# Groups of seven products in the first gate and up block of FFN 2 and in the embedding's first pair of blocks, and six tiles for the heads' squares

## The chip, the cores and the metric

The kernel runs on one core of one Trainium2 chip. The metric is the device time of one execution in microseconds (us); lower is better. Before the change three runs took 1833.35, 1833.89 and 1834.02 us.

The core's engines work beside one another: TensorE (PE in the profile; its weight loads are PEld), VectorE (DVE), ScalarE (ACT), GpSimd (POOL) and SyncE (SP). SP issues most DMA transfers; POOL issues a few, among them the accumulating ones, which add into what they write. The on-chip memory is SBUF; TensorE writes its sums to PSUM.

## The reference, cut to what matters

One layer of a streaming encoder: 256 tokens, width 2048, everything in float32.

```python
x = x + 0.5 * swiglu(rms_norm(x, ffn1_norm), ffn1_w_gate, ffn1_w_up, ffn1_w_down)
h = rms_norm(x, mix_norm); proj = h @ w_in            # u | q | k | v
y_ssm = s5_mixer(u, ...)                              # with a gated linear unit at its end
y_sb = stick_breaking_attention(rms_norm(q), rms_norm(k), v)
x = x + concatenate([rms_norm(y_ssm), rms_norm(y_sb)]) @ w_out
x = x + 0.5 * swiglu(rms_norm(x, ffn2_norm), ffn2_w_gate, ffn2_w_up, ffn2_w_down)
gate = sigmoid(rms_norm(x, ple_norm) @ w_ple_gate)    # the embedding: 2048 x 2048
x = x + rms_norm((p @ w_ple_proj) * gate, ple_post_norm)
```

with `swiglu(h, g, u, d) = (silu(h @ g) * (h @ u)) @ d` and an inner width of 5632.

## The kernel before, in words

**Products in three passes.** Each float32 operand is split into a high part (rounded, by a cast on ACT, line 181) and a low part (what is left, a subtraction on DVE, line 184). A product is the sum of high x high, low x high and high x low: three matmuls where one would do in a lower precision. Weights come as quarters: four rows of 128 inputs by 512 columns, 1 MB in one `raw` tile. There are five such tiles; two of them hold `x` from time to time, and during the embedding all the time. A quarter is split in two halves of 128x1024 elements, into tiles `whi` and `wlo` (four of each; while a pool for sums is open, three more, `shi` and `slo`).

**Blocks.** The 256 tokens are two tiles of 128 rows. A block is 512 columns of output for all tokens, its inner dimension taken a quarter at a time: 2048 inputs are quarters 0 to 3. `gemm_half` (line 315) issues 12 matmuls of 128x128 by 128x512 for one half. `gemm_block` does one block; `gemm_pair` does two blocks with quarters 0 and 1 of the first, 0 and 1 of the second, then quarter 2 of each, then quarter 3 of each.

**Groups of seven products.** The class `Seven` (line 463) handles two blocks together, gate and up for instance. For one quarter, activations and weights make two 2x2 matrices of blocks, and the products of the two matrices are formed in Winograd's way, from seven products and some additions, not eight. The seven are numbered 1 to 7, and are issued in the order 1, 5, 6, 4, 2, 3, 7. `chunk` (line 504) loads both weight quarters, forms three sums of weights on DVE (`add`, line 501), a fourth by an accumulating DMA from SBUF to SBUF on POOL's queue (line 525, for product 7), and splits the seven weight operands. The sums of activations, called forms, are made once per quarter by `whole_rows` (line 443) and `sum_forms` (line 458). `column` does ordinary quarters for one of the two blocks into the same PSUM banks. The banks 1, 2, 4 and 5 are `acc` tiles of 512 columns (four exist); 6 and 7 share one `aux` tile of 1024 columns, 3 and 8 the other (two exist). A group thus uses all of PSUM, and afterwards `opened` and `gated` combine its banks by additions on DVE and a copy on ACT; a last addition takes in banks 3 and 8 (line 622).

In FFN 2's gate and up products, blocks 1 to 10 each use two groups (quarters 0 and 1) and ordinary columns for quarters 2 and 3. Block 0 uses `gemm_pair` and no group; after its gate half, the forms of quarters 0 and 1 are made for the later blocks. The embedding's gate blocks 0 and 1 use `gemm_pair`, and ACT applies the sigmoid right from PSUM (`gate_block`).

**Around these places.** `Normed` holds the normalised, transposed input: a block of `x` is turned on DVE (line 216), sent through SBUF by 16 small DMAs on SP's queue (line 229), and split with the gain (lines 191 and 193). The row scale from the mean of squares comes later, at the evacuation. In the mixer, the heads' outputs and the gated unit's outputs are squared and summed by `add_square`: ACT squares into a tile `sqp` (two exist), POOL adds it to a total (line 1331). Of the totals `rms` makes a row scale (a sum by TensorE, small DVE operations, a square root on ACT), with which line 1464 evacuates the output projection's blocks.

**What sets the order.** The program is written with work put off by so many steps (`put_off`, `step`), and a planner then orders each engine's instructions by the program's order and by when it reckons that their inputs and tiles are there. Instructions wrapped in `pin` keep the program's order. At run time each queue is served in the planned order.

Of the kernel before, what the change touches and what calls it, by code (L numbers as in the profile page):

```python
# [33 lines left out]
def layer_kernel(ctx: ExitStack, tc: tile.TileContext, a: dict, shapes: dict, out: bass.AP):  # L34
# [32 lines left out]
    def get(pool, tag, width=1024, bufs=1):  # L67
        return pool.tile([P, width], F32, tag=tag, name=uid(tag), bufs=bufs)
# [486 lines left out]
    def ffn(i, xn, nxt, bg=None):  # L555
# [23 lines left out]
        for f in range(NF):  # L579
            if prep and f == early:  # L580
# [3 lines left out]
                sevens = pools.enter_context(sums_phase(f"sums{i}"))  # L584
                hp = pools.enter_context(phase(f"h{i}b"))
                sums = [sum_forms(sevens, whole_rows(sevens, xn(kb)), "h") for kb in range(2)]
            if sevens and f:
                sg, hh = com("sg"), com("h")
                gate_cols, up_cols = ([u[:, t * NB : (t + 1) * NB] for t in range(TT)] for u in (sg, hh))

                def opened(s, g=gate_cols, u=up_cols):
                    nc.scalar.copy(g[0], s.bank(1))
                    nc.vector.tensor_tensor(out=u[0], in0=s.bank(6), in1=g[0], op=ALU.add)
                    nc.vector.tensor_tensor(out=u[1], in0=s.bank(7), in1=u[0], op=ALU.add)

                def gated(s, g=gate_cols, u=up_cols, hh=hh):
                    for z, (ps, other) in enumerate(((s.bank(2), g[0]), (s.bank(4), u[1]))):
                        nc.vector.tensor_tensor(out=g[z], in0=ps, in1=other, op=ALU.add)
                        nc.scalar.activation(g[z], g[z], AF.Silu, scale=xn.rs(z))
                    v = hh.rearrange("p (t n) -> p t n", t=TT)  # L600
                    nc.vector.tensor_tensor(
                        out=v, in0=s.bank(5).unsqueeze(1).to_broadcast([P, TT, NB]), in1=v, op=ALU.subtract
                    )

                s = Seven(xn, lambda kb: sums[kb], ((wg, f * NB), (wu, f * NB)), sevens)
                two = f != early
                if f == early:
# [12 lines left out]
                put_off(0, gated, s)  # L620
                s.column(1, (2, 3) if two and f != early else (1, 2, 3), True)
                nc.vector.tensor_tensor(out=hh, in0=s.banks[3.8], in1=hh, op=ALU.add)
# [12 lines left out]
            if f == 0 and bg:  # L635
                warm_up(10)
                first = first_quarters(wg, xn)
            if f == 0 and not bg:
                both = gemm_pair(xn, ((wg, 0), (wu, 0)), KD)
                pg = next(both)  # L640
                sums = [sum_forms(sevens, whole_rows(sevens, xn(kb))) for kb in range(2)]
            else:
                pg = gemm_block(xn, wg, f * NB, KD, first)
            sg = com("sg")
            if f == 0 and bg:
# [6 lines left out]
            pu = gemm_block(xn, wu, f * NB, KD) if f or bg else next(both)  # L652
            if prep and f == 0:
                start(prep)
            hh = com("h")
# [669 lines left out]
    def add_square(pool, total, src, first):  # L1325
        if first:
            nc.scalar.activation(total, src, AF.Square)
        else:
            sq = get(pool, "sqp", T, 2)
            nc.scalar.activation(sq, src, AF.Square)  # L1330
            nc.gpsimd.tensor_tensor(out=total, in0=total, in1=sq, op=ALU.add)

# [180 lines left out]
            ple(n, t, gate, ps[t])  # L1513

    wg = a["w_ple_gate"][0]
    g0, g1 = (gate_block(ps) for ps in gemm_pair(npl, ((wg, 0), (wg, NB)), KD))
    proj_block(0, g0)
    proj_block(1, g1)
    proj_block(2, gate_block(gemm_block(npl, wg, 2 * NB, KD)))
    n = ND - 1  # L1520
    gate = com("h")
    gates = gemm_resident(npl, a["w_ple_gate"][0], n * NB, KD, fin, KD - 8)
    projs = gemm_resident(lambda k: pT, a["w_ple_proj"][0], n * NB, PD // P, fin, PD // P, 2)

    def add(t, n_, r):
        x, g = xt[t][n_], es[n_][:, t * NB : (t + 1) * NB]
# [54 lines left out]
    diag = fin.tile([P, P], F32, name="diag")  # L1581
# [96 lines left out]
```

## Time and profile before

| | |
|---|---|
| three runs | 1833.35, 1833.89, 1834.02 us (median 1833.89) |
| the profiled execution's own time | 1833.81 us |
| its span, from first to last instruction | 1831.7 us |
| TensorE busy | 1820.2 us, 8972 matmuls |
| VectorE busy | 1506.1 us |
| ScalarE busy | 1047.8 us |
| GpSimd busy | 95.7 us |
| granted TensorE clock | 0.999 |

The profile is of one execution. Times in its rows are microseconds from the span's start. A row of the timeline has the start, the duration, engine, line of the kernel, operation, output <- inputs, shape and count; in brackets stands how long the engine was idle before it, and what ended that wait. A matmul's duration includes its way through the array, so that neighbours overlap: their cost is the distance from start to start. Rows by stretch give the stretch, its length, and the busy time of each engine with its instructions, then the granted clock, the share of DMA busy and GB/s.

### The profile page before, as it was taken

The numbers are of one execution on the slowest core, as the hardware profiler recorded it, in microseconds if no ns is written. First come the engines' busy times: TensorE is split into PE (matmuls) and PEld (weight loads), VectorE is DVE, ScalarE is ACT, GpSimd is POOL, SyncE is SP. The second block draws the span as 40 slices with busy tenths as digits, with TensorE's granted clock in tenths as the row PEclk, the third lists the DMA queues.
The fourth block names the chain that finished last, engine by engine and source line by source line (L and its number), as shares of the span: only waits on it lengthen the run. The fifth ranks groups of instructions, "written<-read, shape, count | busy, mean of one in ns | idle before, by whom it ended". The sixth has DMA issues, their size and how long they took to land.

```text
span 1831.7 us, 24182 instructions
## 1 busy us (share of the span) xinstructions
PE 1820.2 (99%) x8972; PEld 1507.0 (82%) x8972; DVE 1506.1 (82%) x1771; ACT 1047.8 (57%) x1221; POOL 95.7 (5%) x145
## 2 busy tenths in 40 slices
PE   9999999999999999999999999999999999999998
PEld 7888888788888888888898888888888888888887
DVE  8967664999999996687566789999999999999565
ACT  7444443655566665365695566555565556666564
POOL 0011000000100000010021000000000010000000
PEclk9999999999999999999999999999999999999999
DMA  9889868677967676675636787887877787767563
GB/s 331 285 271 289 253 209 252 207 236 227 281 215 247 207 238 216 191 265 170 209 132 215 227 300 213 258 253 248 244 221 239 240 267 235 235 205 248 176 214 127
DMA packets 237639, 425.79 MB, mean 232 GB/s; under 512 B 27376, under 2 KB 51312, under 8 KB 237232
## 3 DMA queue, kind: packets, MB, share of 16 engines
q1 hardware_dynamic: 227824, 392.81, 64.6%
q0 software_dynamic: 8976, 30.02, 7.5%
q8 instruction: 70, 1.15, 0.2%
q10 hardware_dynamic: 720, 1.41, 0.2%
q14 instruction: 49, 0.40, 0.1%
HBM read 373.46 MB, written 11.93 MB: 210 GB/s over the span
## 4 chain that ended last, share of the span: by engine, by line
PE 91%; DVE 5%; DMA 2%; issue 1%; ACT 1%; SPq 0%; DVEq 0%; ACTq 0%
PE acc L322 18%; PE acc L327 18%; PE acc L323 18%; PE aux L323 6%; PE aux L322 6%; PE aux L327 6%; PE acc L497 3%; PE acc L494 3%; PE acc L495 3%; PE aux L497 2%; PE aux L494 2%; PE aux L495 2%; DVE wlo L184 1%; DVE slo L184 1%; DMA raw<-in_ffn_w_down 1%
## 5 line engine op out<-in xcount | busy, mean ns | idle before, releaser
L184 DVE TENSOR_TENSOR wlo<-raw,whi 128x1024 fp32r<-128x1024 f32 x496 | 600.4, 1222 | 201.0 <-ACT whi L181 192.9
L181 ACT CAST whi<-raw 128x1024 fp32r<-128x1024 f32 x496 | 515.1, 1051 | 382.7 <-PE acc L323 256.5
L322 PE MATMUL acc<-whi,nhi 128*128 128x512 f32 x1132 | 443.5, 392 | 2.0 <-ACT whi L181 1.6
L323 PE MATMUL acc<-whi,nlo 128*128 128x512 f32 x1132 | 440.8, 389 | 0.0
L327 PE MATMUL acc<-wlo,nhi 128*128 128x512 f32 x1132 | 309.8, 389 | 0.2 <-DVE wlo L184 0.2
L322 PEld LDWEIGHTS acc<-whi,nhi 128*128 128x128 f32 x1132 | 212.5, 188 | 48.2 <-ACT whi L181 2.4
L327 PEld LDWEIGHTS acc<-wlo,nhi 128*128 128x128 f32 x1132 | 212.4, 188 | 44.8 <-DVE wlo L184 0.6
L323 PEld LDWEIGHTS acc<-whi,nlo 128*128 128x128 f32 x1132 | 212.6, 188 | 43.3
L184 DVE TENSOR_TENSOR slo<-raw,shi 128x1024 fp32r<-128x1024 f32 x170 | 207.0, 1218 | 19.3 <-ACT shi L181 18.9
L181 ACT CAST shi<-raw 128x1024 fp32r<-128x1024 f32 x170 | 178.5, 1050 | 66.8 <-DMA raw<-in_ffn_w_down 27.1
L181 ACT CAST whi<-sum 128x1024 fp32r<-128x1024 f32 x65 | 68.5, 1053 | 121.5 <-DVE sum L501 105.6
L181 ACT CAST shi<-sum 128x1024 fp32r<-128x1024 f32 x46 | 48.5, 1054 | 81.9 <-DVE sum L501 74.0
L501 DVE TENSOR_TENSOR sum<-sum,raw 128x1024 f32<-128x1024 f32 x74 | 90.3, 1220 | 0.5
L184 DVE TENSOR_TENSOR wlo<-sum,whi 128x1024 fp32r<-128x1024 f32 x65 | 79.4, 1222 | 4.9 <-ACT whi L181 4.1
L525 POOL DMA_DIRECT2D raw<-raw x37 | 32.1, 869 | 908.6 <-DVE sum L501 550.7
L322 PE MATMUL acc<-whi,hhi 128*128 128x512 f32 x188 | 73.1, 389 | 0.0
L323 PE MATMUL acc<-whi,hlo 128*128 128x512 f32 x188 | 73.1, 389 | 0.0
L184 DVE TENSOR_TENSOR hlo<-hT,hhi 128x1024 fp32r<-128x1024 f32 x56 | 68.2, 1217 | 2.6 <-ACT hhi L181 2.5
L181 ACT CAST hhi<-hT 128x1024 fp32r<-128x1024 f32 x56 | 58.6, 1046 | 5.2 <-PE aux L327 2.8
L322 PE MATMUL aux<-whi,hhi 128*128 128x512 f32 x156 | 60.7, 389 | 0.0
L323 PE MATMUL aux<-whi,hlo 128*128 128x512 f32 x156 | 60.7, 389 | 0.0
L184 DVE TENSOR_TENSOR slo<-sum,shi 128x1024 fp32r<-128x1024 f32 x46 | 56.2, 1221 | 1.2 <-ACT shi L181 0.8
(373 smaller groups left out, 3071.2 us busy)
## 6 DMA issues: line engine op xcount, KB each, us to landing
raw<-in_ffn_w_up SPq DMA_DIRECT2D x88, 1024.0 KB, 5.9
raw<-in_ffn_w_down SPq DMA_DIRECT2D x88, 1024.0 KB, 5.2
raw<-in_ffn_w_gate SPq DMA_DIRECT2D x86, 1024.0 KB, 7.9
raw<-in_w_in SPq DMA_DIRECT2D x32, 1024.0 KB, 5.6
raw<-raw POOLq DMA_DIRECT2D x37, 512.0 KB, 5.7
raw<-in_w_out SPq DMA_DIRECT2D x16, 1024.0 KB, 5.1
raw<-in_w_ple_gate SPq DMA_DIRECT2D x16, 1024.0 KB, 5.1
hT<-mid SPq DMA_DIRECT2D x160, 64.0 KB, 4.2
```

What stands on the lines that cost most here:

```text
L181: copy = nc.scalar.copy(hi, src)
L184: nc.vector.tensor_tensor(out=lo, in0=src, in1=hi.bitcast(F32), op=ALU.subtract)
L322: nc.tensor.matmul(ps[t], lhsT=lh, rhs=hi[:, j, cols], start=start and j == 0, stop=False)
L323: nc.tensor.matmul(ps[t], lhsT=ll, rhs=hi[:, j, cols], start=False, stop=False)
L327: nc.tensor.matmul(ps[t], lhsT=lh, rhs=lo[:, j, cols], start=False, stop=stop and j == 1)
L494: nc.tensor.matmul(ps, lhsT=lh[j], rhs=hi[:, j], start=begin and j == 0, stop=False)
L495: nc.tensor.matmul(ps, lhsT=ll[j], rhs=hi[:, j], start=False, stop=False)
L497: nc.tensor.matmul(ps, lhsT=lh[j], rhs=lo[:, j], start=False, stop=z in final and j == 1)
L501: nc.vector.tensor_tensor(out=t, in0=x, in1=y, op=ALU.add)
L525: nc.gpsimd.dma_start(b12, b22, accum_op=ALU.add)
```

## The change

FFN 2's block 0 becomes one group of seven: ordinary columns of quarter 1 for gate and up, the group for quarter 0 (whose products 1, 5, 6 and 7 are complete with it), and columns of quarters 2 and 3. The forms of quarter 0 now stand ahead of the block, those of quarter 1 behind its gate columns. The combining by `opened` and `gated` is that of the other blocks.

The embedding's blocks 0 and 1 become ordinary columns of quarter 0, groups for quarters 1 and 2, and columns of quarter 3, with their own `opened`, `gated`, pool for sums and forms. The resident weights and one small tile of the last block move from the pool `fin` to a pool `own`, opened after the pool for sums is closed. The tiles `sqp` become six.

```diff
-            if sevens and f:
+            if sevens:
...
-                if f == early:
+                if f == 0:
+                    sums = [sum_forms(sevens, whole_rows(sevens, xn(0)))]
+                    s.column(0, (1,))
+                    s.column(1, (1,))
+                    s.chunk(0, shared)
+                    put_off(0, opened, s)
+                    s.column(0, (2,))
+                    s.column(1, (2,))
+                    s.column(0, (3,), True)
+                    sums.append(sum_forms(sevens, whole_rows(sevens, xn(1))))
+                elif f == early:
...
-                s.column(1, (2, 3) if two and f != early else (1, 2, 3), True)
+                s.column(1, (3,) if f == 0 else (2, 3) if two else (1, 2, 3), True)
...
-            if f == 0 and not bg:
-                both = gemm_pair(xn, ((wg, 0), (wu, 0)), KD)
-                pg = next(both)
-                sums = [sum_forms(sevens, whole_rows(sevens, xn(kb))) for kb in range(2)]
-            else:
-                pg = gemm_block(xn, wg, f * NB, KD, first)
+            pg = gemm_block(xn, wg, f * NB, KD, first)
...
-            sq = get(pool, "sqp", T, 2)
+            sq = get(pool, "sqp", T, 6)
...
-    g0, g1 = (gate_block(ps) for ps in gemm_pair(npl, ((wg, 0), (wg, NB)), KD))
+    g0, g1 = (com("h") for _ in range(2))
+    h0, h1 = ([g[:, t * NB : (t + 1) * NB] for t in range(TT)] for g in (g0, g1))
+
+    def opened(s):
+        nc.scalar.copy(h0[0], s.bank(1))
+        nc.vector.tensor_tensor(out=h1[0], in0=s.bank(6), in1=h0[0], op=ALU.add)
+        nc.vector.tensor_tensor(out=h1[1], in0=s.bank(7), in1=h1[0], op=ALU.add)
+
+    def gated(s):
+        for t, (ps, other) in enumerate(((s.bank(2), h0[0]), (s.bank(4), h1[1]))):
+            nc.vector.tensor_tensor(out=h0[t], in0=ps, in1=other, op=ALU.add)
+            sigmoid(g0, t, h0[t])
+        v = g1.rearrange("p (t n) -> p t n", t=TT)
+        nc.vector.tensor_tensor(
+            out=v, in0=s.bank(5).unsqueeze(1).to_broadcast([P, TT, NB]), in1=v, op=ALU.subtract
+        )
+
+    with sums_phase("sums3") as sevens:
+        forms = {}
+        s = Seven(npl, lambda kb: forms[kb], ((wg, 0), (wg, NB)), sevens)
+        forms[1] = sum_forms(sevens, whole_rows(sevens, npl(1)), "h")
+        s.column(0, (0,))
+        s.column(1, (0,))
+        s.chunk(1)
+        forms[2] = sum_forms(sevens, whole_rows(sevens, npl(2)), "h")
+        s.chunk(2, shared)
+        put_off(0, opened, s)
+        s.column(0, (3,), True)
+        put_off(0, gated, s)
+        s.column(1, (3,), True)
+        nc.vector.tensor_tensor(out=g1, in0=s.banks[3.8], in1=g1, op=ALU.add)
+        for t in range(TT):
+            sigmoid(g1, t, h1[t])
+    own = ctx.enter_context(phase("own"))
...
-    gates = gemm_resident(npl, a["w_ple_gate"][0], n * NB, KD, fin, KD - 8)
-    projs = gemm_resident(lambda k: pT, a["w_ple_proj"][0], n * NB, PD // P, fin, PD // P, 2)
+    gates = gemm_resident(npl, a["w_ple_gate"][0], n * NB, KD, own, KD - 8)
+    projs = gemm_resident(lambda k: pT, a["w_ple_proj"][0], n * NB, PD // P, own, PD // P, 2)
```

More of the change, by code (lines that the diff above doesn't have):

```diff
@@ L634, in ffn @@
             first = ()
-            if f == 0 and bg:
+            if f == 0:
                 warm_up(10)
                 first = first_quarters(wg, xn)
-            if f == 0 and not bg:
-                both = gemm_pair(xn, ((wg, 0), (wu, 0)), KD)
-                pg = next(both)
-                sums = [sum_forms(sevens, whole_rows(sevens, xn(kb))) for kb in range(2)]
-            else:
-                pg = gemm_block(xn, wg, f * NB, KD, first)
+            pg = gemm_block(xn, wg, f * NB, KD, first)
             sg = com("sg")
-            if f == 0 and bg:
+            if f == 0:
                 for n in range(ND):
@@ L651, in ffn @@
                 gate()
-            pu = gemm_block(xn, wu, f * NB, KD) if f or bg else next(both)
+            pu = gemm_block(xn, wu, f * NB, KD)
             if prep and f == 0:
@@ L1580, in layer_kernel @@
     pin(nc.vector.scalar_tensor_tensor(out=r, in0=tmp, scalar=-3.0, in1=r, op0=ALU.add, op1=ALU.mult))
-    diag = fin.tile([P, P], F32, name="diag")
+    diag = own.tile([P, P], F32, name="diag")
     nc.scalar.activation(diag, ident, AF.Copy, scale=r)
```

## The prediction

> **What bounds the kernel now.** I read the page first: busy times, the 40 slices, the chain that ended last.
>
> ```profile
> span 1831.7 us, 24182 instructions
> PE 1820.2 (99%) x8972; PEld 1507.0 (82%) x8972; DVE 1506.1 (82%) x1771; ACT 1047.8 (57%) x1221; POOL 95.7 (5%) x145
> DVE  8967664999999996687566789999999999999565
> PE 91%; DVE 5%; DMA 2%; issue 1%; ACT 1%; SPq 0%; DVEq 0%; ACTq 0%
> ```
>
> TensorE is in the chain for 91% of the span and hardly waits, so a removed matmul is worth its start-to-start time. But VectorE is at nine tenths in every slice that runs groups of seven products. So I asked for busy time by stretch: FFN 2's first block, its second block (two groups), and the embedding's first pair, with the splits' low parts (line 184) of that pair alone, and VectorE alone in the stretch ahead of the pair.
>
> ```profile
> 1039.00:1082.50 43.50, 43.50 (x194) 36.03 (x193) 33.76 (x47) 27.23 (x37) 1.99 (x3) 1.00 0.81 273
> 1082.50:1123.30 40.80, 40.80 (x182) 33.80 (x181) 39.95 (x39) 25.07 (x26) 1.75 (x2) 1.00 0.78 236
> 1723.50:1767.20 43.70, 43.70 (x194) 36.22 (x193) 24.82 (x33) 26.27 (x32) 0.00 (x0) 1.00 0.63 213
> ...
> 1723.50:1767.20 43.70, 19.97 (x17) 1.00 0.63 213
> ...
> 1702.00:1723.90 21.90, 11.40 (x12) 1.00 0.70 241
> ```
>
> After the stretch's length come PE, PEld, DVE, ACT, POOL. FFN 2's second block has VectorE busy for 39.95 of 40.80 us and TensorE still never waits: groups are paid for in VectorE time, and there the purse is nearly empty. The stretches that the change touches have 9.7 and 18.9 us of it left.
>
> **Matmuls removed.** From the timeline of PE, the first matmul of FFN 2's first group and the first one behind it:
>
> ```profile
> 1082.71 0.39 PE L494 MATMUL acc<-whi,hhi 128*128 128x512 f32 x1
> ...
> 1092.23 0.39 PE L322 MATMUL acc<-whi,nhi 128*128 128x512 f32 x1
> ```
>
> A group has 7 x 6 = 42 matmuls: 9.52 / 42 = 0.227 us each. The quarter that it replaces has 4 halves x 12 = 48. Each group saves 6 x 0.227 = 1.36 us of TensorE; three groups, 4.08.
>
> **VectorE work added.** A group has seven splits for four and three additions: +6 operations of 128x1024. Its products need combining: two adds in `opened`, two adds and one wide subtraction in `gated`, one wide add at the end. Each new set of row forms takes a sum, four quarter operations and a low part. Paces (back to back, start to start) from DVE's timeline, and the row forms from the chain:
>
> ```profile
> 1669.22 1.22 DVE L184 TENSOR_TENSOR slo<-raw,shi 128x1024 fp32r<-128x1024 f32 x1
> 1670.36 1.22 DVE L184 TENSOR_TENSOR wlo<-raw,whi 128x1024 fp32r<-128x1024 f32 x1
> ...
> 1656.47 0.68 DVE L674 SCALAR_TENSOR_TENSOR x<-sg,x 128x512 f32<-128x512 f32 x1
> 1657.07 0.68 DVE L674 SCALAR_TENSOR_TENSOR x<-acc,x 128x512 f32<-128x512 f32 x1
> ...
> 322.44 1.11 DVE rows L458 x3
> ```
>
> So 1.14 us for 1024 elements, 0.60 for 512, 0.37 for a quarter form: 6.8 per group, 3.5 for `opened` and `gated`, 3.8 per set of forms.
>
> *FFN 2's first block.* Its forms are no new work, and the first set even moves ahead. Before, its cast stood at 1059.11, though its rows were done at 1016.66:
>
> ```profile
> 1016.24 0.42 DVE L458 TENSOR_TENSOR rows<-whole,rows 128x256 f32<-128x256 f32 x1
> ...
> 1059.11 1.03 ACT L181 CAST nhi<-rows 128x1024 fp32r<-128x1024 f32 x1
> ...
> 1073.40 1.22 DVE L501 TENSOR_TENSOR sum<-raw,raw 128x1024 f32<-128x1024 f32 x1
> ```
>
> I read that 43 us as tiles of one kind being given out in the program's order, behind the last normalised quarter; now the forms come ahead of it. VectorE's 33.76 us held work for the next block: from 1073.40 on, eight operations, 9.1 us. The rest, 24.7, grows by 6.8 + 3.5 to 35.0, in a window of 43.5 - 1.36 = 42.1 us. It fits; the lead on the next block shrinks from 9.1 to at most 7.1 us. SP carries the same eight weight loads in another order, and POOL one more accumulating DMA, not due before the seventh product, 8.2 us into the group. ACT adds three casts and a copy to 27.23 of 43.5: hidden, unless VectorE is late. So -1.36 us.
>
> Against it: the block's up-sums now take the first of the two wide PSUM tiles, and the next block's third product needs that one, 12 matmuls (2.72 us) after the next block starts. It is freed by the 1.22 us add on line 622, which in today's boundaries starts this long after the next block's first matmul:
>
> ```profile
> 1123.51 0.39 PE L494 MATMUL acc<-shi,hhi 128*128 128x512 f32 x1
> 1123.71 1.22 DVE L622 TENSOR_TENSOR h<-aux,h 128x1024 f32<-128x1024 f32 x1
> ...
> 1368.34 0.39 PE L494 MATMUL acc<-whi,hhi 128*128 128x512 f32 x1
> 1371.64 1.22 DVE L622 TENSOR_TENSOR h<-aux,h 128x1024 f32<-128x1024 f32 x1
> ```
>
> 0.2 to 3.3 us; it may start 1.5 late at no cost. The wait is 0 to 1.8. I take +0.3, since TensorE's order can place another product there. Sum for the block: -1.06, from -1.36 to +0.44.
>
> *The embedding's pair.* VectorE's 24.82 us contain 16 low parts (17 rows with the 0.7 us one for p), three of them for the blocks behind the pair (3.7 us), as three of the pair's own stood ahead of it. What must run before the last low part: 24.8 - 3.7, + 2 x 6.8 for the groups, + 3.8 for the second forms (the first fit ahead of the pair), + 3.5, less 13 x 0.08 as isolated operations close up: 41.0 us. Can it start early? The second forms stand behind the first group's additions in the two tiles for sums, by the order read above. The first addition wants the fourth load, and the rows below show what VectorE does when FFN 2 ends.
>
> ```profile
> 1723.73 0.39 PE L322 MATMUL acc<-whi,nhi 128*128 128x512 f32 x1
> ...
> 1767.26 0.39 PE L322 MATMUL acc<-whi,pT 128*128 128x512 f32 x1
> ...
> 1723.94 0.69 DVE L674 SCALAR_TENSOR_TENSOR x<-aux,x 128x512 f32<-128x512 f32 x1 [0.86 <-PE aux L327]
> ...
> 1734.33 0.53 SPq L312 DMA_DIRECT2D raw<-in_w_ple_gate  x1
> ...
> 1740.06 1.05 ACT L181 CAST whi<-raw 128x1024 fp32r<-128x1024 f32 x1 [5.10 <-DMA raw<-in_w_ple_gate]
> ```
>
> From 1723.94, 41.0 us end at 1764.9; the last low part is due 8 matmuls (1.8 us) before the pair's end. So VectorE lets the pair end no sooner than 1766.7, though TensorE alone would come from 1767.26 to 1764.5. With 0.4 idle (half of the 0.85 in the full block above) 1767.1: -0.1 of the hoped -2.72. TensorE waits about 2.6 us, in the second group. That group also wants two loads at once: the fifth (issued 1734.33, landed 1740.06, behind twelve turning DMAs on SP) and the sixth, about 3 us behind it; it starts at 1744.1. Bounds: -2.72 (all covered) and +2.3 (below). ACT's 26.27 us grow by eight casts and a copy to about 35 of 41, and POOL, idle there, issues two accumulating DMAs: hidden behind VectorE. The other move (the last block's tiles from a pool opened later) is hidden: its memory was free two blocks earlier; uncovered it costs one split, a cast of 1.05 and a low part of 1.14, 2.2 us.
>
> **Six tiles for the squares.** Views: the timelines of PE, ACT, POOL, DVE around 970, and the adds' line 1331.
>
> ```profile
> 970.99 0.39 PE L327 MATMUL acc<-wlo,nhi 128*128 128x512 f32 x1
> 973.21 0.47 PE L322 MATMUL acc<-whi,nhi 128*128 128x512 f32 x1 [1.15 <-ACT whi L181]
> ...
> 966.82 0.39 ACT L1330 ACTIVATE sqp<-aux 128x256 f32<-128x256 f32 x1 [0.48 <-DVE sm L1319]
> 968.56 0.38 ACT L1330 ACTIVATE sqp<-aux 128x256 f32<-128x256 f32 x1 [1.08 <-POOL sqa L1331]
> 969.38 0.38 ACT L1330 ACTIVATE sqp<-aux 128x256 f32<-128x256 f32 x1 [0.43 <-POOL sqa L1331]
> 971.07 0.20 ACT L203 ACTIVATE sm<-sm 128x2 f32<-128x2 f32 x1
> ...
> 967.85 0.70 DVE L201 TENSOR_SCALAR sm<-sm 128x2 f32<-128x2 f32 x1
> 971.31 0.17 DVE L204 RECIPROCAL sm<-sm 128x2 f32<-128x2 f32 x1 [2.76 <-ACT sm L203]
> 972.31 0.75 DVE L1464 SCALAR_TENSOR_TENSOR x<-acc,sm,x 128x512 f32<-128x512 f32 x1
> ...
> L1331 POOL TENSOR_TENSOR sqa<-sqa,sqp x7: 738/1221/1699, 929.1 to 970.2; 128x256 f32<-128x256 f32 x7
> ```
>
> The four low-part matmuls from 970.99 end in pace at 971.90; the next one starts at 973.21: 1.31 us lost. Two waits of ACT for POOL (1.08 + 0.43 = 1.51) hold up the square root at 971.07; five small DVE operations and the evacuation at 972.31 follow, which frees PSUM; the cast that the row names fits as well, and both stand behind the waits. With six tiles no wait is left: everything comes 1.51 earlier, and the gap closes: -1.31. But POOL's own adds do not move (the last starts at 970.2), so the five small operations now run beside them, as the one at 967.85 did: 0.70 us, against 0.17 for its neighbour at 971.31. One such delay, 0.53, less the 0.2 to spare (1.51 - 1.31), leaves -1.0. Bounds: -1.5 (slow restarts gone too) and 0.
>
> [...]
>
> **Sum.** -1.06 - 0.1 - 1.0 = -2.16 on the profiled 1833.81: 1831.65; the median shown stands 0.08 above it: **1831.7**. That is inside 0.2% (3.7 us), about what a measurement of this kernel can tell from no change.
>
> **Rivals.** Full gain: the embedding's second forms and sums slip into the idle 10 us ahead of the pair, so VectorE is no bound there. 4.08 + 1.31: 1828.5, up to 1830.2 with the waits above. For: TensorE never waits in the 97% block. Against: the 43 us that the cast waited. 0.26.
>
> POOL keeps the square root late: the small operations wait out the last add, from the rows 970.2 + 0.74, then four operations of 0.2 and 0.9 to the matmul as from 972.31 to 973.21, so 972.65: a gain of 0.55, or 0.4 with one more turn. 1832.3. For: the 0.70 us row. Against: only one operation of its kind shows it. 0.12; that the six tiles do nothing at all (another wait behind 970.99) ends 0.4 higher and is counted here. [...]
>
> Slower: FFN 2's VectorE never regains its lead. Once the next block's additions start under about 3 us ahead, the accumulating DMA comes late and each block stalls, as one did in FFN 1:
>
> ```profile
> 416.02 7.96 DMA raw<-raw
> ...
> 426.19 0.50 PE L494 MATMUL acc<-whi,nhi 128*128 128x512 f32 x1 [0.37 <-ACT whi L181]
> ```
>
> About a microsecond went there. Five of ten blocks at 1.2 make 6 us: 1837.7. For: 0.85 us idle in the second block. Against: 7.1 us of lead remain by the count. 0.10.
>
> The DMA decides the embedding's second group: sixth load at 1743, its sum done at 1745.4, 7.96 + 0.9 for the DMA, 2.2 for the split: the seventh product's low part at 1756.4 instead of 1752.7; VectorE, held at that split, idles about 2.4 more. Pair +2.3: 1834.1, the upper part of my case's own range.
>
> **How the numbers follow.** My case, VectorE as the embedding's bound, 0.52 (alone 1830.3 to 1834.1); full gain 0.26; POOL 0.12; slower 0.10. The range 1828.9 to 1834.6 leaves out the lowest part of full gain (0.06), the slower case (0.10) and a little of mine. Faster by over 0.2% is full gain (0.26); slower 0.09; the rest 0.65.
>
> **What would show it.** Matmuls 8972 - 18 = 8954. No gap behind 970.99, or one under 1 us. In the embedding's pair VectorE near 95% busy, with TensorE waiting for low parts or sums in the second group; if it runs gapless in 41 us, my step on the order of tiles is wrong. FFN 2's third product of block two shows a wait for line 622 or none. Waits on `raw<-raw` in several blocks would make it slower.

## The result, and the profile after

The changed kernel takes 1839.47 us (median of 7 runs, 1836.92 to 1843.12); the kernel before took 1834.02 beside it (median of 7, 1833.04 to 1835.59). The ratio is 1.0027, 95% interval 1.0018 to 1.0037: slower by 0.27%, with an interval wholly above 1. The forecast was 1831.7, and its range ended at 1834.6.

The profiled execution of the changed kernel took 1836.92 us with a span of 1835.2, 3.5 us above the span before. The page's first rows, and VectorE's 40 slices:

```profile
span 1835.2 us, 24216 instructions
PE 1817.8 (99%) x8954; PEld 1503.2 (82%) x8954; DVE 1542.0 (84%) x1813; ACT 1057.3 (58%) x1234; POOL 97.2 (5%) x148
DVE  8957664999999996687567899999999998989795
```

The 18 matmuls are gone, and TensorE is busy for 2.4 us less; the span is longer by 3.5, so TensorE now waits some 6 us more. The starts of each stage's first matmul in the two timelines say where:

| stage (us) | before | after | difference |
|---|---|---|---|
| start to FFN 2's block 0 | 1039.19 | 1037.85 | -1.34 |
| FFN 2's block 0 | 43.52 | 42.16 | -1.36 |
| FFN 2's blocks 1 to 10 and down products | 641.02 | 643.53 | +2.51 |
| embedding's first pair | 43.52 | 47.17 | +3.65 |
| rest | 64.44 | 64.43 | 0 |

The first row is no measure of the six tiles: in the profiles of this kernel and of those below that have them too, and whose text is the same in this stretch, it lasts 1037.85 to 1041.18 us.

Busy time by stretch in the profile of after, for FFN 2's block 0 and the embedding's pair (after the stretch's length: PE, PEld, DVE, ACT, POOL, the granted clock, the share of DMA busy, GB/s):

```profile
1037.85:1080.01 42.16, 42.16 (x188) 34.91 (x186) 40.79 (x55) 28.11 (x38) 2.88 (x4) 1.00 0.88 284
1723.54:1770.71 47.17, 42.70 (x181) 34.28 (x180) 45.66 (x60) 32.78 (x39) 1.73 (x2) 0.96 0.67 208
```

Block 0 went as hoped. In the pair VectorE is busy for 45.66 of 47.17 us, TensorE for 42.70, and its clock was not whole. TensorE's timeline of the pair has two waits, both at the start of the second group (of its products 5 and 6):

```profile
1749.05 0.79 PE L494 MATMUL acc<-shi,hhi 128*128 128x512 f32 x1 [3.59 <-ACT shi L181]
1749.65 0.63 PE L495 MATMUL acc<-shi,hlo 128*128 128x512 f32 x1
1750.07 0.63 PE L494 MATMUL acc<-shi,hhi 128*128 128x512 f32 x1
...
1752.86 0.50 PE L494 MATMUL aux<-whi,hhi 128*128 128x512 f32 x1 [0.88 <-ACT whi L181]
```

Start to start, they cost 3.75 and 1.28 us more than pace (0.227 us a matmul); and behind the first, matmuls start 0.43 us apart, which comes to 1.2 us more. That is 6.2 of the 6.37 us that 180 matmuls at pace (40.80) lack to 47.17.

What the waits are for, in the timelines of ACT and then of VectorE:

```profile
1747.95 1.05 ACT L181 CAST shi<-sum 128x1024 fp32r<-128x1024 f32 x1 [0.54 <-DVE sum L501]
```

```profile
1723.74 1.29 DVE L679 SCALAR_TENSOR_TENSOR x<-aux,x 128x512 f32<-128x512 f32 x2 [0.86 <-PE aux L327]
1724.95 1.22 DVE L443 TENSOR_TENSOR whole<-nhi,nlo 128x1024 f32<-128x1024 f32 x1
...
1731.07 1.22 DVE L184 TENSOR_TENSOR hlo<-rows,hhi 128x1024 fp32r<-128x1024 f32 x1
...
1742.24 1.22 DVE L443 TENSOR_TENSOR whole<-nhi,nlo 128x1024 f32<-128x1024 f32 x1
...
1746.64 1.22 DVE L501 TENSOR_TENSOR sum<-raw,raw 128x1024 f32<-128x1024 f32 x1
```

The reader is to see three things. VectorE does not pause from 1723.74 to the second group's first sum at 1746.64: its queue has 22.9 us of work ahead of that sum. Both sets of forms lie in that stretch, the first at 1724.95, behind FFN 2's last evacuation (line 679), and not in the idle time ahead of it. And the sum is what the group waits for: its cast follows at 1747.95 and product 5 at 1749.05, 2.41 us behind the sum. Ahead of product 5 stand 96 matmuls (48 of columns, 42 of the first group, 6 of product 1), 21.8 us; so the sum had to start 19.4 us into the pair, and started 23.1 us into it.

Six tiles: in the profile of after, the matmul behind the four low parts follows 1.14 us behind the first of them, 0.24 over pace where 1.31 had been:

```profile
970.72 1.07 PE L327 MATMUL acc<-wlo,nhi 128*128 128x512 f32 x4
971.86 0.47 PE L322 MATMUL acc<-whi,nhi 128*128 128x512 f32 x1
```

In FFN 2, block 1 lasts 41.53 us and block 7 43.03, where the pace gives 40.80; the other eight keep it within 0.02. Block 7's chain of waits and ACT's queue in it:

```profile
1340.50 8.88 DMA raw<-raw
...
1349.53 1.06 ACT shi L181
1350.61 1.23 DVE slo L184
1351.83 1.14 DVE wlo L184
```

```profile
1342.16 1.05 ACT L181 CAST whi<-sum 128x1024 fp32r<-128x1024 f32 x1 [0.19 <-DVE sum L501]
1349.53 1.05 ACT L181 CAST shi<-raw 128x1024 fp32r<-128x1024 f32 x1 [6.31 <-DMA raw<-raw]
1350.48 1.04 ACT L181 CAST whi<-sum 128x1024 fp32r<-128x1024 f32 x1
```

The same block before, on ACT:

```profile
1347.52 1.06 ACT L181 CAST whi<-sum 128x1024 fp32r<-128x1024 f32 x1 [1.46 <-DVE sum L501]
1348.48 1.05 ACT L181 CAST whi<-raw 128x1024 fp32r<-128x1024 f32 x1
1352.03 1.05 ACT L181 CAST whi<-raw 128x1024 fp32r<-128x1024 f32 x1 [2.50 <-DMA raw<-raw]
```

The accumulating transfer took about as long in both (8.9 us after, 9.6 before). Before, the cast that waits for it stood behind the sum's; after, the planner put it ahead of that one. ACT stands for 6.31 us, the sum of 1345.45 waits for its cast until 1350.48, and TensorE with it.

### The profile page after: what moved, and what is told of

Same layout as the page of the kernel before. It is cut to its first block, busy times and chain, and to the rows that moved or that the text cites. A ratio compares the mean times of both kernels' runs of the same rounds, so it can differ in the third digit from the quotient of the medians.

```text
span 1835.2 us, 24216 instructions
## 1 busy us (share of the span) xinstructions
PE 1817.8 (99%) x8954; PEld 1503.2 (82%) x8954; DVE 1542.0 (84%) x1813; ACT 1057.3 (58%) x1234; POOL 97.2 (5%) x148
## 3 DMA queue, kind: packets, MB, share of 16 engines
q8 instruction: 70, 1.15, 0.3%
## 4 chain that ended last, share of the span: by engine, by line
PE 94%; DVE 3%; DMA 1%; ACT 1%; issue 0%; SPq 0%; DVEq 0%; ACTq 0%
PE acc L322 17%; PE acc L327 17%; PE acc L323 17%; PE aux L323 7%; PE aux L322 7%; PE aux L327 7%; PE acc L497 4%; PE acc L495 4%; PE acc L494 4%; PE aux L497 3%; PE aux L494 3%; PE aux L495 3%; DVE wlo L184 1%; DMA raw<-raw 0%; DVE slo L184 0%
## 5 line engine op out<-in xcount | busy, mean ns | idle before, releaser
L322 PE MATMUL acc<-whi,nhi 128*128 128x512 f32 x1056 | 413.9, 392 | 2.3 <-ACT whi L273 1.8
L323 PE MATMUL acc<-whi,nlo 128*128 128x512 f32 x1056 | 411.2, 389 | 0.0
L327 PE MATMUL acc<-wlo,nhi 128*128 128x512 f32 x1056 | 290.2, 389 | 0.2 <-DVE wlo L184 0.2
L322 PEld LDWEIGHTS acc<-whi,nhi 128*128 128x128 f32 x1056 | 198.2, 188 | 45.4 <-ACT whi L273 2.7
L327 PEld LDWEIGHTS acc<-wlo,nhi 128*128 128x128 f32 x1056 | 198.1, 188 | 41.9 <-DVE wlo L184 0.6
L323 PEld LDWEIGHTS acc<-whi,nlo 128*128 128x128 f32 x1056 | 198.3, 188 | 40.3
L181 ACT CAST shi<-raw 128x1024 fp32r<-128x1024 f32 x177 | 185.4, 1048 | 65.9 <-DMA raw<-in_ffn_w_down 23.2
L184 DVE TENSOR_TENSOR slo<-sum,shi 128x1024 fp32r<-128x1024 f32 x54 | 66.0, 1223 | 3.2 <-ACT shi L181 2.5
L322 PE MATMUL acc<-whi,hhi 128*128 128x512 f32 x164 | 63.8, 389 | 0.0
L323 PE MATMUL acc<-whi,hlo 128*128 128x512 f32 x164 | 63.8, 389 | 0.0
L322 PE MATMUL aux<-whi,nhi 128*128 128x512 f32 x156 | 60.7, 389 | 0.0
```

The source lines that it names most:

```text
L181: copy = nc.scalar.copy(hi, src)
L184: nc.vector.tensor_tensor(out=lo, in0=src, in1=hi.bitcast(F32), op=ALU.subtract)
L322: nc.tensor.matmul(ps[t], lhsT=lh, rhs=hi[:, j, cols], start=start and j == 0, stop=False)
L323: nc.tensor.matmul(ps[t], lhsT=ll, rhs=hi[:, j, cols], start=False, stop=False)
L327: nc.tensor.matmul(ps[t], lhsT=lh, rhs=lo[:, j, cols], start=False, stop=stop and j == 1)
```

## Experiments

Stages as in the table above; "pair" is the embedding's first pair, "wait" what TensorE first loses against pace in its second group by half a microsecond or more (at product 5, in e15 at product 4). The ratio is to the kernel before, run beside each.

| run | block 0 | blocks 1 to 10, down | pair | wait | ratio |
|---|---|---|---|---|---|
| after | 42.16 | 643.53 | 47.17 | 3.75 | 1.0027 [1.0018, 1.0037] |
| e1_no_ple | 42.16 | 644.27 | 43.52 | | 0.9999 [0.9990, 1.0008] |
| e2_ple_only | 43.52 | 640.64 | 49.37 | 4.22 | 1.0026 [1.0016, 1.0036] |
| e3_one_group | 42.16 | 642.57 | 42.16 | | 0.9990 [0.9981, 0.9998] |
| e4_sqp_only | 43.52 | 642.94 | 43.52 | | 1.0000 [0.9991, 1.0009] |
| e5_own_raws | 42.16 | 643.60 | 49.47 | 3.3 | 1.0029 [1.0019, 1.0039] |
| e6_one_set | 42.16 | 643.11 | 45.19 | 2.38 | 1.0005 [0.9995, 1.0014] |
| e9_both | 42.16 | 643.69 | 45.39 | 2.49 | 1.0010 [1.0001, 1.0019] |
| e7_filled | 42.16 | 643.48 | 48.66 | 0.5, then 1.7 | 1.0024 [1.0013, 1.0034] |
| e10_no_forms | 42.16 | 643.14 | 44.06 | 0.8 | 0.9994 [0.9984, 1.0004] |
| e8_ffn_as_before | 43.52 | 640.59 | 42.16 | | 0.9985 [0.9977, 0.9994] |
| e12_one_group_again | 42.16 | 643.79 | 42.16 | | 0.9992 [0.9982, 1.0001] |
| e11_ffn_only | 42.16 | 642.92 | 43.52 | | 1.0001 [0.9993, 1.0009] |
| e13_pool_load | 42.16 | 643.41 | 49.82 | 3.83 | 1.0032 [1.0021, 1.0043] |
| e14_pool_load_one_set | 42.16 | 643.84 | 43.77 | 0.8 | 0.9996 [0.9987, 1.0005] |
| e15_pool_load_no_forms | 42.16 | 643.00 | 45.90 | 3.53 | 1.0005 [0.9996, 1.0013] |
| e16_pool_load_ffn_as_before | 43.52 | 640.63 | 48.32 | 2.89 | 1.0016 [1.0006, 1.0026] |

For the loss in the pair the theories were that VectorE's queue is late (two sets of forms inside the pair), that the second group's loads are late, or both; for FFN 2, that its group is a gain, or that the blocks behind it give the gain back.

### Which part costs the time

The changed kernel with the embedding's pair as before; only the embedding's part; only one group in the pair; only the six tiles.

```diff
# e1_no_ple: the embedding's groups taken out
-    with sums_phase("sums3") as sevens:
...
+    g0, g1 = (gate_block(ps) for ps in gemm_pair(npl, ((wg, 0), (wg, NB)), KD))
# e3_one_group: quarter 2 as ordinary columns
-        s.chunk(1)
-        forms[2] = sum_forms(sevens, whole_rows(sevens, npl(2)), "h")
-        s.chunk(2, shared)
+        s.chunk(1, shared)
         put_off(0, opened, s)
+        s.column(0, (2,))
+        s.column(1, (2,))
# e2_ple_only and e4_sqp_only: the kernel before, with the other parts left as they were there
```

> The embedding's pair as before (plain pair of blocks); FFN 2's group and the six tiles stay. Theory A (the loss is made in the embedding's second group, whose start waits for its second load and for VectorE, and in the slower clock behind that wait): the pair is back at 43.5 us, the runs come close together again, and the time is 1834.0 - 1.1 (tiles) - 1.4 (FFN 2's group) + 0 to 2 for the gaps seen in FFN 2's blocks 1 and 7: 1831.5 to 1833.5. Rival B (FFN 2's VectorE lost its lead and the blocks stall): still above 1835, with new gaps in FFN 2.

> Only the embedding's two groups; FFN 2 and the two tiles as before. Theory A: all of the loss and more is here: the pair takes about 47 us or more instead of 43.5, the time is 1837.5 to 1843 and spread over several us. Rival B: within 1 us of before or faster by up to 2.7.

> The embedding with one group (quarter 1) and ordinary columns for quarters 0, 2 and 3; all else as in the changed kernel. VectorE has some 10 us less to do in the pair. Theory A: no wait over 1 us in the pair, which takes 42.2 us, and the time is about 1.3 under the kernel without any group in the embedding. If a group in the embedding starves whatever VectorE has to do (its two loads at once with three raw tiles), the pair still waits 2 us or more.

> Only six tiles for the squares. By the gap seen in the changed kernel (0.47 instead of 1.54 us between the same two matmuls): 1.1 us faster, 1832.9. If it is worth 1.3 or more, the small operations are not held by GpSimd's adds; if it is worth under 0.5, they are.

The embedding's part alone is as slow as the whole change (1.0026), and without it the change is neither faster nor slower (0.9999). With one group in place of two the pair runs without a wait: 42.16 us, 1.36 less than before, as one group should give. So the second group is the loss. The six tiles close the gap behind the heads' evacuation in each profile that has them (0.24 us left), about a microsecond, which the run times of e4 (1834.48 against 1834.44) don't show. Its profiled execution, at 1837.76 the slowest of its eleven, lost 1.14 and 1.24 us in blocks 7 and 10 of FFN 2, whose order the planner had changed too.

### The second group: whose lateness?

A tile of its own for each of the second group's two weight loads (e5), so that they need not wait for an old one; the first group's forms used in both (e6), so that the second set is not computed; both (e9); and the wait filled with matmuls that add zero (e7).

```diff
# e5_own_raws
...
-                raw = wp.tile([P, 4, NB], F32, tag="raw", name=uid("raw"), bufs=5)
+                raw = own.tile([P, 4, NB], F32, name=uid("own")) if own else wp.tile(
+                    [P, 4, NB], F32, tag="raw", name=uid("raw"), bufs=5)
...
-        s.chunk(2, shared)
+        s.chunk(2, shared, sevens)
# e6_one_set
-        forms[2] = sum_forms(sevens, whole_rows(sevens, npl(2)), "h")
+        forms[2] = forms[1]
# e7_filled, behind product 1 of the second group; zero is a tile of zeros
...
+                for i in range(fill):
+                    nc.tensor.matmul(
+                        self.bank(5), lhsT=zero, rhs=parts[0].rearrange("p j t -> p (j t)")[:, :NB],
+                        start=False, stop=False,
+                    )
...
-        s.chunk(2, shared)
+        s.chunk(2, shared, 16)
```

> The changed kernel, with the second group's two weight quarters in two tiles of their own, so that their loads wait for no earlier split. Theory A (VectorE's queue: in the changed kernel's trace the group's first sum starts at 1746.64 right behind other VectorE work, with no idle time before it): the wait ahead of the second group's second product stays at 3 to 4 us, the pair at 46.5 to 49 us. Rival C (the raw tile: the sixth load went out only at 1740.12, after the first group's split of the same tile at 1738.84): the wait falls under 1.5 us and the pair under 45.

> The changed kernel without the second set of row forms: the second group multiplies the first group's forms, so VectorE does 3.8 us less and ScalarE one cast less; part of the gate's result is left out. Theory A alone: the wait of 3.75 us falls to about 0. Rival C alone: stays at 3 us or more. Both (VectorE's queue first, the late load behind it, landing at about 1745.4 at the earliest): falls by some 1.2 us, to 2 to 2.7.

> Tiles of their own for the second group's loads, and no second set of forms (part of the gate's result is left out). If VectorE's queue and the late load together make the wait: it goes away (under 0.5 us), TensorE's clock stays whole, and the pair takes 41 to 42.5 us. If there is a third cause, a wait of over 1 us remains.

> The changed kernel with 16 matmuls of zero weights (16 x 0.227 = 3.6 us) in front of the second group's second product, in the place of the wait. Theory D (the spread and some us of the loss come from TensorE's clock, which falls to half behind a wait of 3.8 us): no matmul at 0.43 us start to start in the pair, pair 45 to 46.5 us, median 1835 to 1837 and the runs within 2 to 3 us of each other, in place of 1839.5 and 6. If the clock has no part: the same time as the changed kernel or up to 3.6 us more, with the same spread.

Own tiles improved nothing (wait 3.3, pair 49.47), and I took that for the end of the loads as a cause. It wasn't: SP's queue in e5 shows both loads from 1738.37 on, still behind twelve of the turning transfers. The later one landed at 1747.18, 22.3 us into the pair, against 21.7 in after; so e5 had not made the loads earlier. One set less took 2.0 us off the pair, not the 3.75 and more that a wait for VectorE alone would give back; something stood behind it. e9 missed for the same reason as e5: its later load landed 21.8 us into the pair, and a wait of 2.49 us stayed. The fill of e7 lengthened the pair by 1.5: the matmuls kept TensorE busy, and the waits of 0.5 and 1.7 us behind them remained, with a half clock at the second (0.50 from 1754 to 1756). The runs spread over 3.6 us (1837.4 to 1841.0), between the 6.2 of the changed kernel and the 2 to 3 expected, which decides nothing about the clock's part in the spread.

### Without any forms

Both groups take the plain rows, so the kernel leaves out the sums of activations, and its gate is not the reference's.

```diff
# e10_no_forms
-        forms[1] = sum_forms(sevens, whole_rows(sevens, npl(1)), "h")
+        forms[1] = npl(1)
...
-        forms[2] = sum_forms(sevens, whole_rows(sevens, npl(2)), "h")
+        forms[2] = npl(2)
```

> The changed kernel without either set of row forms in the embedding's pair: the two groups take the plain rows in their place, so the summed rows of the gate are left out and the computation is changed; the same matmuls, loads and splits stay, VectorE has twelve operations and 7.6 us less. Theory 'VectorE's queue alone': with one set left out the second group's first sum started 21.7 us into the pair and TensorE waited 2.38 us; 3.8 us less again puts it at about 18, ahead of the 19.5 at which it would come too late. The wait is gone or under 0.5 us, the granted clock stays whole, the pair takes 40.8 to 41.5 us (47.17 in the changed kernel), the time is about 6 us under that of the changed kernel. Rival 'a third cause' (the loads, ScalarE's casts, or the planner's order): the second group still waits 2 us or more, the clock falls to half behind it, the pair takes 44 us or more.

A miss: 44.06 us and not 41, with waits of 0.8, 0.2, 0.8 and 0.9. VectorE's queue is no longer the cause there. VectorE's timeline of e10, at the split that frees the sixth load's tile and at the second group's first sum, and SP's at that load:

```profile
1736.51 1.22 DVE L184 TENSOR_TENSOR wlo<-raw,whi 128x1024 fp32r<-128x1024 f32 x1
...
1744.94 1.23 DVE L501 TENSOR_TENSOR sum<-raw,raw 128x1024 f32<-128x1024 f32 x1 [3.80 <-DMA raw<-in_w_ple_gate]
```

```profile
1737.82 0.52 SPq L511 DMA_DIRECT2D raw<-in_w_ple_gate  x1
```

VectorE idles for 3.8 us until the load lands at 1744.9, 20.1 us into the pair and 7.1 behind its issue. On SP thirteen of the sixteen turning transfers (line 229) come ahead of it. They were not the only hold: the load goes into an old tile, which that split gave up at 1737.73, just when SP came to the load. In the changed kernel the tile was the later of the two by half a microsecond (split from 1738.84 to 1740.06, load at 1740.12). So queue and tile held the load almost equally long, and to free one of them, as e5 and e9 did, moved nothing.

### The load taken off SP

Now both holds go: the second group's loads are issued on GpSimd's queue, into own tiles: with all forms (e13), with one set (e14), with none (e15), and with all forms and FFN 2 as before (e16).

```diff
# e13_pool_load, on top of e5_own_raws; e14 adds e6's edit, e15 adds e10's
-                nc.sync.dma_start(
+                (nc.gpsimd if own else nc.sync).dma_start(
```

> The changed kernel with tiles of its own for the second group's two weight quarters in the embedding's pair, loaded on GpSimd's queue and so ahead of the turning transfers on SP. Theory 'both' (VectorE's queue and the load each hold the second group): VectorE works without a pause up to that group's first sum as before, so the sum stays at about 23 us into the pair and TensorE waits 3 us or more; pair 46 to 47.5 us. Theory 'the load alone': the sum comes at about 19 us, the wait goes, the pair takes about 41 us.

> The same, and the second group takes the first group's row forms, so that its own set is left out (the gate's second group is computed with the wrong rows). With the load on SP this waited 2.38 us, the pair took 45.19. Theory 'both': the sum no longer waits for the load, VectorE has 3.8 us less ahead of it, so it comes at about 19.5 us into the pair; the wait is under 1 us, the clock stays whole, pair 41 to 42.5 us. Theory 'VectorE's queue alone': no change from 45.19, since there the load didn't matter.

> The same with no row forms in the embedding's pair at all (both groups take the plain rows, the gate is computed wrong). With the load on SP the pair took 44.06 us with waits of 2.67. Theory 'both': nothing holds the second group any more; waits under 0.5 us, pair 40.8 to 41.5. If the waits stay, it is neither of the two, but ScalarE's order or the accumulating transfer.

The loads now start at 1714.47 and 1720.44 (e13), and with a median of 6.3 us from issue to landing have long landed. In e13 nothing improves: VectorE, again without a pause, comes to the sum 23.2 us into the pair. (The pair, at 49.82, is even longer than the 46 to 47.5 expected, as is that of e16: the half clock lasted longer, see below.) VectorE's timeline of e13, and then of e14 at the same sum:

```profile
1748.46 1.22 DVE L501 TENSOR_TENSOR sum<-own,own 128x1024 f32<-128x1024 f32 x1
1749.60 1.22 DVE L184 TENSOR_TENSOR hlo<-rows,hhi 128x1024 fp32r<-128x1024 f32 x1
...
1745.38 1.22 DVE L501 TENSOR_TENSOR sum<-own,own 128x1024 f32<-128x1024 f32 x1
```

So in the changed kernel it is VectorE's queue, and the load alone is excluded. In e14 the sum comes at 19.4, the longest wait is 0.8, the clock stays whole and the pair takes 43.77 (41 to 42.5 was expected), where the same forms with the load on SP took 45.19, and 45.39 into own tiles: there the load was the bound. In e15, with neither, the group was to run through, and doesn't: 45.90 us. The timelines of ACT and of TensorE in e15:

```profile
1742.72 1.05 ACT L181 CAST whi<-own 128x1024 fp32r<-128x1024 f32 x1
1748.04 1.04 ACT L181 CAST whi<-own 128x1024 fp32r<-128x1024 f32 x1 [4.26 <-DMA own<-own]
1748.99 1.04 ACT L181 CAST whi<-raw 128x1024 fp32r<-128x1024 f32 x1
1749.94 1.04 ACT L181 CAST shi<-sum 128x1024 fp32r<-128x1024 f32 x1
```

```profile
1751.03 0.79 PE L494 MATMUL acc<-shi,nhi 128*128 128x512 f32 x1 [3.37 <-ACT shi L181]
```

It is block 7's wait once more: the cast for product 7 stands in ACT's queue ahead of the one for product 4 (at 1749.94), and waits 4.26 us for the accumulating transfer, issued at 1739.73, which took 8.2 us. So three bounds lie one behind the other in that group: VectorE's queue, the load (its place on SP and its tile), and the order of ACT's casts around the accumulating transfer. The first decides in the changed kernel.

### What FFN 2's group is worth

One group in the pair and the six tiles, without FFN 2's group (e8) and with it (e12, which is e3 again); FFN 2's group alone (e11).

```diff
# e8_ffn_as_before: e3_one_group, and in ffn
-            if sevens:
+            if sevens and f:
...
# e11_ffn_only: e1_no_ple, and
-            sq = get(pool, "sqp", T, 6)
+            sq = get(pool, "sqp", T, 2)
```

> The six tiles and one group of seven in the embedding's first pair (as in the experiment with one group); FFN 2's first block as in the kernel before. Theory 'FFN 2's gain is given back in the blocks behind it': first block 43.5 us, blocks 1 to 10 and the down products near 641.0 in place of 642.6 to 644.3, so the time is within 1 us of the kernel with one group and FFN 2's group, and about 2.4 us under the kernel before (-1.07 for the six tiles, -1.36 for the group). Rival 'FFN 2's group is a gain, and the gaps behind it come from elsewhere': 1.4 us slower than the kernel with one group and FFN 2's group.

> The kernel with one group in the embedding's pair, FFN 2's group and the six tiles once more, on the same chip as the kernel without FFN 2's group. 42.16 us for FFN 2's first block, 42.16 for the pair, 1 to 2 us under the kernel before. Theory 'given back': within 1 us of the kernel without FFN 2's group. Rival 'FFN 2's group is a gain': 1.4 us under it.

> FFN 2's group alone, without the embedding's groups and with two tiles for the squares. Theory 'given back': first block 42.16 us, the same gaps in the first and seventh of the blocks behind it (0.5 and 1.8 us), time 0 to +1.2 us against the kernel before. Rival 'it is a gain': about -1.36 us, and no gaps in blocks 1 to 10.

> All forms, the second group's loads on GpSimd's queue, the six tiles, and FFN 2's first block as in the kernel before. Theory 'both': the pair costs 46 to 47.5 us as in the first of these, blocks 1 to 10 are without the new gaps, time 0.5 to 1.5 us over the kernel before. Theory 'the load alone': pair about 41, time 1830.5, faster than the version with one group (1831.6).

Without FFN 2's group 1831.62, with it 1833.10 (12 runs each on the same chip; the kernel before 1834.56): as medians go, the group loses about 1.5 us rather than gaining 1.36; the two intervals overlap. e13 and e16 differ the same way (1841.10 with it, 1838.01 without, on one chip), while e11, the group alone, is level with the kernel before (1.0001). So the group gains nothing, and how much it loses the run times leave open. The profiles agree: in all thirteen with the group, blocks 1 to 10 take 2.0 to 3.7 us over pace, always with 1.6 to 2.7 in block 7; of the five without it four take at most 0.5, and e4 2.4, in other places (early in block 7, and in block 10). e16 shows the same split, 640.63 in FFN 2 and 48.32 in the pair. e8, at 0.9985 [0.9977, 0.9994], is the fastest version of this case: 0.15% under the kernel before, with an interval wholly below 1.

## Why the prediction was wrong

The sum was -1.06 - 0.1 - 1.0 = -2.16 on the profiled time; the profiled execution lost 3.1, and the median 5.5. Between the sum and the profiled span lie 5.6 us: 3.75 of them in the embedding's pair (forecast -0.1, measured +3.65) and 2.2 in FFN 2 (forecast -1.06, measured +1.15), less 0.3 in the rest.

**Matmuls and six tiles: right.** 8954 matmuls, 1.36 us a group where the group runs unhindered (block 0; the pair in e3). The gap of 1.31 shrank to 0.24: 1.07, predicted 1.0. POOL's adds still run up to 970.7, beside the five small operations, as the step said. Two of the five took longer than before, not one: line 206's took 0.40 us (0.16 before), and line 208's 0.60 (0.17), until 970.73, while POOL's last add ended at 970.71:

```profile
970.13 0.60 DVE L208 TENSOR_SCALAR sm<-sm 128x2 f32<-128x2 f32 x1
```

That is 0.67 us of delay where 0.53 was counted; the square root, for its part, came 1.7 us earlier against the matmuls, not 1.51. The two errors about cancel.

**The embedding's pair: the step that failed.** It is the clause "the first fit ahead of the pair". VectorE was taken to have 41.0 us of work in the pair; with the first set of forms inside it, 3.8 more, it was 44.8. From 1723.74, VectorE's first row of the pair, and with the same 1.8 us at the end, that gives 1770.3; the pair ended at 1770.71. VectorE did idle ahead of the pair, so there was room. VectorE alone, after:

```profile
1702.00:1723.54 21.54, 12.25 (x13) 1.00 0.62 206
```

It was busy for 12.25 of the last 21.54 us, and the operands of the first set had been there since 1640. But the planned order has the first set behind line 679, which waited for TensorE, and VectorE stood idle for those 0.86 us (the row of 1723.74) and took the set only behind it, at 1724.95. I had read from block 0 that tiles are given out in the program's order, used this for the second set, and not for the first. What put the set there (the tiles for sums, or the planner's estimate) was not tried.

The agreement of the two sums hides a second flaw: the bound wasn't at the pair's end. From 1752.86 on TensorE ran at pace to the end. VectorE decided at the second group's first sum, due at 19.4 us and there at 23.1. The count of work up to that point, and not the total, is the right test. e14, which has the VectorE work that I had counted and no load in the way, took 43.77, against the 43.0 to 43.4 that the prediction's ends give; so with the first set ahead of the pair, the term would have been about right, if the load had been there as well.

It hadn't. The DMA rival named this: "VectorE, held at that split, idles about 2.4 more. Pair +2.3". The place was one step off (the sixth load and the sum, not the split of product 7), the size near: e6, with one set and the load on SP, took 1.67 us more than before. In the changed kernel this bound was hidden under VectorE's: the load landed at 1745.25, 1.4 us ahead of the sum.

**The clock: a term that was missing.** Behind the wait TensorE went at half pace (0.43 us from start to start in place of 0.227), for which the sum had no term. The rows by stretch of TensorE alone, of after:

```profile
1748.00:1750.00 2.00, 0.95 (x2) 0.68 0.07 14
1750.00:1752.00 2.00, 1.98 (x5) 0.50 1.08 205
1752.00:1754.00 2.00, 1.14 (x5) 0.97 0.23 43
```

(After the length: PE busy, granted clock, DMA share, GB/s.) The granted clock is 0.50, for about 3.4 us. In e2, e16 and e13, each with a second wait of 1.3 to 1.45 us inside the slow stretch, that lasted 6.8, 6.8 and 10.2 us. The same view of e13:

```profile
1752.00:1756.00 4.00, 3.12 (x8) 0.50 0.52 98
1756.00:1760.00 4.00, 4.00 (x11) 0.50 0.00 0
```

There the pair is 2.65 longer than that of after, and the mean granted clock of the span 0.997. The changed kernel's seven runs have 0.999 in the two shortest (1836.92, 1837.37) and 0.996 or 0.997 in the others (1838.81 to 1843.12). By that likeness the profiled execution was one of the milder ones, and the rest of the 5.5 us may be a longer stretch at half clock. That is not shown: no profile of such a run of the changed kernel itself was taken, and runs of the kernel before spread as widely with a clock of 0.999 or 1.000 (beside e13, 1832.73 to 1839.39).

**FFN 2: right in the block, wrong behind it.** Block 0 took 42.16, and VectorE was busy 40.79 of them, in line with 35.0 and a lead of up to 7. The wait for line 622's tile, costed at 0.3, did not come: the add, now line 632, started 2.5 us into block 1, within the 0 to 3.3 read from before, and no matmul waited for it. The cost came from the slower rival, "VectorE never regains its lead", in part: two of ten blocks, 0.73 and 2.23 us, not five of 1.2. Block 1's wait is for a low part, as a shorter lead would have it. Block 7's is the planner's order on ACT; why it planned so is not settled, only that it did so in every profile with the group. The prediction had the accumulating transfer's 7.96 us in a row, and did not ask which casts stand behind it on ACT. The -1.36 became +1.15 in the profile of after (-1.36 and +2.51).

**The other rivals.** Full gain did not occur; its premise, the second forms in the idle time ahead of the pair, was further off than the case that I took. POOL keeping the square root late showed in one operation, but too early in the row of small operations to cost what the rival said: line 208's ended 0.02 us behind the last add, and one operation was left behind it (0.24 us of gap, not 0.76).

## What to carry to other kernels

Where an engine's queue is nearly full, count its work up to each point at which another engine needs a result, in the queue's order; a total over the stage, or idle time ahead of it, says nothing of an operation that stands behind a waiting one. Taking one bound away shows the next only if you look at what the late instruction waited for then: here three lay in one group, each worth 2.4 to 3.8 us of wait where it decided (e6, e15, e13), and a tile of its own did not move a load that its queue held (e5: landed 22.3 us into the pair, against 21.7). And cast operands that wait for a slow transfer last on their engine: one such wait in the wrong place, 6.31 us of ACT in block 7, cost 2.23 us, where a group of seven products saves 1.36.

## What the runs showed of the hardware that I had not expected

In the embedding's pair every wait of 2.38 us or more was followed by half the granted clock (down to 0.50 to 0.53 in the rows by stretch): 2.38 us in e6, 2.49 in e9, 2.89 in e16, 3.3 in e5, 3.53 in e15, 3.75 in after, 3.83 in e13, 4.22 in e2. Ahead of it, in after, TensorE had been busy for 393.28 of 393.60 us (from 1351.50) at a granted clock of 1.00. The next matmuls started 0.43 us apart, in after and e6 at once, in e16 after four more at full pace; in e5 the clock was still 1.00 from 1750 to 1752, with five matmuls in it, and 0.57 in the 2 us after that. In e7 two waits of 0.5 and 1.7 us, 2.3 us apart, did the same. Single waits of 0.8 us (e10, e14), of 1.35 us (after, block 7 of FFN 2) and of 1.52 us (before, ahead of the matmul of 337.00) left the clock at 1.00. The stretch at half clock lasted 3.4 us in after and e6, 6.8 in e2 and e16, 10.2 in e13; each of the longer ones, two and three times 3.4 us, has a second wait of 1.3 to 1.45 us in it. The second wait of after, 1.28 us, began in the slow stretch and ended behind it (the clock was 0.97 from 1752 to 1754). How long a wait must be for the clock to fall, and what sets the length of the slow stretch, no run shows.

An accumulating transfer of 512 KB from SBUF to SBUF has a median of 5.3 us from issue to landing in after, and single ones took 8.88 (block 7) and 8.2 (e15); in the kernel before, the one issued at 1342.32 in block 7 took 9.6.
